# List-scheduling both attentions of a hybrid decoder with their transfers, and moving half of a second output projection into the attention ahead of it

## The chip, the cores and the metric

The kernel runs on one core of one Trainium2 chip. The metric is the device time of one execution in microseconds (us). A core has a matrix engine, TensorE (PE; its weight loads are shown as PEld), a vector engine (DVE), a scalar engine (ACT), a general engine, GpSimd (POOL), and SyncE (SP), whose queue issues all transfers of this kernel.

## What is computed

A decoder trunk of two layers over 1024 tokens of width 1024, in float32:

```python
for l in range(2):
    h = rms_norm(x, attn_norm[l])
    if l == 0:   # 12 heads of 64 in 2 groups: compressed, selected and window branch, gated sum
        o_mix, q_mem = nsa_mixer(h, a_w_in, ...)
    else:        # 12 heads: causal softmax over q k^T + decay, K, V and gates from one shared projection
        hs = rms_norm(x, kv_norm) @ w_kv_shared
        o_mix, q_mem = forgetting_attention(h @ b_w_in, hs), ...
    o_mem = memory_attention(q_mem, mem, ...)          # 4 heads over 256 memory tokens
    x = x + concat(o_mix, o_mem) @ w_o[l]
    x = x + conv_ffn(rms_norm(x, ffn_norm[l]), ...)    # 1024 -> 2 x 2816, conv of 3, gate, -> 1024
return rms_norm(x, final_norm)
```

With 1024 tokens there are 16 blocks to select from and 16 are selected, so the selected branch is plain causal attention.

## The kernel before

**Products.** Every float32 operand is split into an upper part (rounded, `hi`, made by ACT) and the rest (`lo`, made by DVE or POOL). `mm3` makes a product of three matmuls, hi x hi, hi x lo, lo x hi (L255 to L257). In attention the two parts of a query or key of 64 rows lie one above the other in one tile of 128 rows, so that two matmuls (`score`, L340) make the three products.

**Stages of the profiled execution**, about: layer 0's projections (0 to 165 us), attention 0 (165 to 600), output projection 0 (to 720), the FFN (to 1400) in a scheme that saves matmuls by sums of blocks, the shared values of layer 1 (to 1480), attention 1 (to 1770), output projection 1 (to 1880), the second FFN and the final norm (to 2506).

**A unit of attention** is one head and one half of the queries (512 columns). Its steps: load the tiles; `score`; `maximum` on DVE (L370, or L357 for a memory head); `exponent` on ACT; `sums` and `normalise`; then per group of key blocks a transpose on PE (`turn_p`, L460), the split of its result (`upper_p`, ACT, L471; `lower_p`, DVE, L474) and the product with the values (`value`, L484). Results go to DRAM (`ob` to `od`, upper and lower part separately), and are loaded, added on POOL and split as operands `oT` of the output projection (`operand`).

**Attention 0** is written by a planner. `Plan` holds tasks with an engine, a cost, what they depend on, a priority, and buffers that they take and give back; `run` simulates the engines and calls the tasks' functions in the order of their simulated starts. PE, ACT, DVE and POOL keep that order. Transfers are tasks of cost 0 on "SP", their landing a fixed delay on the dependency (4 to 9 us), and SP's instructions stand where the framework puts them. `SHIFT` moves single tasks' priorities. Between the units' tasks stand, as filler for PE, the projections of queries to come (`rope_tasks`, `plain_tasks`), and from unit -8 on one half of the output projection (`half`): the k-tiles 0 to 3 (`EARLY`) by the first 512 columns, added to `x` and stored as `xh`. `out_proj` then does the other four k-tiles for these columns, and all eight for the rest. The attention's normalising is POOL's (L424 to L428).

**Attention 1** (`attention`) follows fixed slots: `pace` sets at which step each group of scores starts, scores are `lead` steps ahead, values `lag` steps behind, and the filler (14 projections of keys and queries, `load_block` and `plain_proj`) is spread evenly up to unit -5. Normalising is DVE's (L430). The weights come with 512-byte rows, and each is split in 8 pieces with its gain (L283 on ACT, L284 on DVE). When the last unit starts, `w_o` is loaded; when the filler is done, an operand is loaded every fourth step, the rest at the end. There is no half product: `out_proj` does eight k-tiles for all columns.

**Transfers.** Parts and heads lie apart in DRAM, so tiles are loaded in pieces: `queries0` 8 DMAs for two tiles, `keys0` 4, a memory unit 4 for its queries (L952), a unit of attention 1 two for `qq`, two for `qx`; a head there two for `kk`, two for `ky`, one for `vv`.

```python
def queries0(self, pool, h, c):
    q = [self.sb(pool, [P, CH], F32R, f"qq{i}", 2) for i in range(2)]
    for i in range(2):
        for half in range(2):
            for x in range(2):
                p0 = (i ^ x) * HD + half * 32
                self.nc.sync.dma_start(f32(q[x][p0:p0 + 32, :]), self.qd0[i, half, h * 32:(h + 1) * 32, c * CH:(c + 1) * CH])
```

Of the kernel before, what the change touches and what calls it, by code (L numbers as in the profile page):

```python
# [18 lines left out]
P = 128  # L19
# [24 lines left out]
class Plan:  # L44
# [20 lines left out]

    def can(self, t):
        free, held = self.free, self.held
        for a in t["acq"]:
            if a == "tp":

                if held.get("tp", 0) > 2 or free["psb"] < (1 if held.get("o") else 2):
                    return False
            elif a == "pb":
                if free["psb"] < 2 or held.get("pb", 0) > (0 if "psa" in held else 1):
                    return False
            elif free["psb" if a == "o" else a] < t["acq"].count(a):
                return False
        return True
# [59 lines left out]
class Trunk:  # L138
# [180 lines left out]
    def score(self, it):  # L319
        nc, br, s = self.nc, it["br"], self.psa()  # L320
        it["s"] = s
        for ii, o, n in it["grp"]:
# [10 lines left out]
            for q, k in zip(br["q"], br["k"]):  # L333
# [77 lines left out]
    def normalise_all(self, u, i0, i1):  # L411
        self.sums(u, i0, i1)
        for br in u["branches"][i0:i1]:
            for ii in br["pt"]:
                self.normalise(br, ii)

# [72 lines left out]
    def pace(steps, items):  # L489


        t = [0.0]
        for st in steps:
            t.append(t[-1] + 0.11 * st["n"] + sum(2 * max(0.11, 0.057 * len(q[2])) for q in st["ps"]))
        size = [0.4 + 0.0012 * sum(n for _, _, n in it["grp"]) for it in items]
        rate, at = t[-1] / sum(size), 10 ** 9
        due, early = 10 ** 9, -10 ** 9
        for it in items:
            early = it["early"] = max(early, it["early"])
        for it, w in reversed(list(zip(items, size))):  # L500
            due = min(due - rate * w, t[it["due"]] if it["due"] >= 0 else it["due"])
            k = int(due) if due < 0 else max(i for i in range(len(steps)) if t[i] <= due)
            at = it["at"] = min(at, max(k, it["early"]))
        assert all(it["early"] <= it["at"] for it in items)

    def attention(self, ap, l, od, units, work, spare, lead=4, lag=2, lead_work=2):
# [3 lines left out]
        units = list(units)  # L510
        steps, items, users = [], [], {}
        for k, u in enumerate(units):
            u["start"] = len(steps)
            steps += self.value_steps(u)
        ends = {id(q[0]): k for k, st in enumerate(steps) for q in st["ps"]}
        for k, u in enumerate(units):
            its, brs = [], u["branches"]
            for br in brs:
                tag, _, bufs = br["p"]
                same = users.setdefault(tag, [])  # L520
                br["early"] = ends[id(same[-bufs])] if len(same) >= bufs else -10 ** 9
                same.append(br)
            scored = brs if len(brs) == 1 else brs[0:2]
            for i, br in enumerate(scored):
                early = max(b["early"] for b in (br, br.get("joint", br)))
                due = next(k for k in range(u["start"], len(steps)) if any(q[0] is br for q in steps[k]["ps"])) - lead
                its += [{"u": u, "br": br, "grp": g, "first": j == 0, "load": False, "early": early, "due": due} for j, g in enumerate(self.groups(br))]
                its[-1]["norm"] = (i, len(brs) if br is scored[-1] else i + 1)
            its[0]["load"] = True
            items += its  # L530
        self.pace(steps, items)
        n_fill = units[-spare]["start"] if spare else len(steps)
        total, owed, done = sum(n for _, n, _ in work), 0.0, set()
        work = [[name, gen] for name, _, gen in work]
        later, halves, whole, oT = {}, [], [], []

        def operand():

            if not oT:
                oT.extend(self.hpair() for _ in range(2))  # L540
            c, kt = whole.pop(0)
            raw = self.wraw([P, 2, CH])
            self.nc.sync.dma_start(raw, od[c][:, kt * P:(kt + 1) * P, :].rearrange("s p q -> p s q"))
            self.nc.gpsimd.tensor_tensor(raw[:, 0], raw[:, 0], raw[:, 1], ALU.add)  # L544
            self.split(raw[:, 0], oT[c][0][:, kt, :], oT[c][1][:, kt, :])

        def after(k, slot, f):
            later.setdefault((k, slot), []).append(f)

        def run(k, slot):  # L550
            for f in later.pop((k, slot), ()):
                f()

        def advance():
            nonlocal total
            total -= 1
            if next(work[0][1], 0) == 0:
                done.add(work.pop(0)[0])

        def begin(k, it):  # L560
            if it["load"]:
                while not set(it["u"]["needs"]) <= done:
                    advance()
                it["u"]["load"]()
            self.score(it)
# [1909 lines left out]
```

## Time and profile before

| | us |
|---|---|
| median of 3 runs | 2505.82 |
| lowest, highest | 2503.11, 2507.7 |
| profiled execution | 2507.87 |
| its span | 2506.1 |
| PE busy | 2439.7 (97%) |
| DVE, ACT, POOL busy | 1839.2, 1347.1, 843.3 |
| chain that ended last: PE, DVE, DMA, ACT | 85%, 5%, 4%, 3% |

The profile is one execution. Busy times are sums over an engine's instructions; a matmul's time runs from its start to its modelled end, and matmuls overlap, so that a full PE shows in how closely they start, not in the busy share alone. "PEclk" is the share of full clock that the matrix engine was granted. A row of waits has the engine, line and tile that waited, who released it, the sum, the number of times and the longest. In a time line, the number in brackets is the idle time ahead of an instruction, with its releaser. "SPq" is SP's queue, where a DMA waits until its buffers are free, and those behind it with it.

### The profile page before, as it was taken

To read this page: it belongs to the slowest core of one execution; us is meant where nothing else is said; L and a number is where in the kernel's file an instruction comes from. 1 tells how busy PE (TensorE), PEld (TensorE's weight loads), DVE (VectorE), ACT (ScalarE), POOL (GpSimd) and SP (SyncE) were. 2 spreads that over 40 slices of the span, in tenths; PEclk is the share of its full clock that TensorE was granted. 3 is DMA by queue.
4 is the path that set the end of the run, shared out by engine and by line. 5 is a ranking of instruction groups with operands and counts; after the bars stand their busy time and mean duration, and the time that the engine had idled before them with its cause. 6 is when DMAs were issued, how large, how long until landed. Compare 5 with 4: busy or idle time off the path is not lost.

```text
span 2506.1 us, 35521 instructions
## 1 busy us (share of the span) xinstructions
PE 2439.7 (97%) x12215; PEld 2048.1 (82%) x12215; DVE 1839.2 (73%) x3066; ACT 1347.1 (54%) x2564; POOL 843.3 (34%) x742
## 2 busy tenths in 40 slices
PE   8989999989999999999999999999999999999998
PEld 7778888877778888888889887887778888888887
DVE  4778777875678777788666477878386788778766
ACT  4458777885354444454455266757244454444444
POOL 2755555584145545520000000000234455451001
PEclk9989999999999999999999999999999999999999
DMA  8663343355423323366336467666622233338423
GB/s 273 231 216 84 98 132 94 109 169 175 148 75 109 105 93 114 101 240 226 101 119 184 150 181 196 181 189 185 208 90 92 97 102 109 101 102 309 169 93 126
DMA packets 290284, 368.18 MB, mean 147 GB/s; under 512 B 30808, under 2 KB 160696, under 8 KB 290104
## 3 DMA queue, kind: packets, MB, share of 16 engines
q1 hardware_dynamic: 290104, 365.91, 46.0%
q8 instruction: 97, 1.59, 0.3%
q14 instruction: 83, 0.68, 0.1%
HBM read 252.38 MB, written 113.45 MB: 146 GB/s over the span
## 4 chain that ended last, share of the span: by engine, by line
PE 85%; DVE 5%; DMA 4%; ACT 3%; issue 2%; POOL 1%; SPq 0%; POOLq 0%; ACTq 0%; DVEq 0%
PE psa L255 13%; PE psa L256 13%; PE psa L257 13%; PE psb L255 10%; PE psb L256 10%; PE psb L257 10%; PE psa L340 6%; PE psb L484 5%; PE psb L460 5%; PE psb L1711 1%; DVE pt L474 1%; ACT pt L471 1%; DMA wr<-in_w_r_dram 1%; ACT ps L383 1%; DVE ps L370 0%
## 5 line engine op out<-in xcount | busy, mean ns | idle before, releaser
L2205 DVE SCALAR_TENSOR_TENSOR v<-u,cw,v 128x1023 f32<-128x1023 f32 (+1 forms) x176 | 274.0, 1557 | 68.8 <-ACT v L2203 68.6
L474 DVE TENSOR_TENSOR pt<-psb,pt 128x512 fp32r<-128x512 f32 (+2 forms) x380 | 244.7, 660 | 81.0 <-ACT pt L471 78.5
L176 ACT ACTIVATE wh<-wr 128x512 fp32r<-128x512 f32 (+1 forms) x210 | 155.7, 742 | 255.4 <-PE psb L257 107.5
L471 ACT ACTIVATE pt<-psb 128x512 fp32r<-128x512 f32 (+2 forms) x380 | 213.9, 576 | 129.8 <-PE psb L460 94.3
L2203 ACT ACTIVATE v<-u,cw 128x1024 f32<-128x1024 f32 x88 | 109.6, 1246 | 310.3 <-DVE u L2192 297.1
L177 DVE TENSOR_TENSOR wl<-wr,wh 128x512 fp32r<-128x512 f32 (+1 forms) x210 | 196.3, 936 | 99.6 <-ACT wh L176 99.2
L484 PE MATMUL psb<-pt,vv 128*128 128x512 f32 (+2 forms) x864 | 249.6, 362 | 8.1 <-DVE pt L474 5.0
L255 PE MATMUL psa<-hT,wh 128*128 128x512 f32 x592 | 231.2, 391 | 4.9 <-ACT rb L1098 3.8
L257 PE MATMUL psa<-hT,wl 128*128 128x512 f32 x592 | 230.6, 390 | 0.0
L256 PE MATMUL psa<-hT,wh 128*128 128x512 f32 x592 | 230.6, 390 | 0.0
L223 POOL TENSOR_TENSOR rs<-ss,consts 128x1 f32<-128x1 f32 x28 | 17.1, 613 | 545.4 <-DVE ss L221 545.4
L340 PE MATMUL psa<-kk,qq 128*128 128x512 f32 (+4 forms) x792 | 176.7, 339 | 6.4 <-DVE stat L370 5.0
L484 PEld LDWEIGHTS psb<-pt,vv 128*128 128x128 f32 x864 | 147.6, 192 | 27.9 <-DVE pt L474 8.7
L383 ACT ACTIVATE ps<-ps,stat 128x128 f32<-128x128 f32 (+1 forms) x192 | 147.4, 770 | 29.7 <-DVE stat L370 28.6
L544 POOL TENSOR_TENSOR wr<-wr 128x512 f32<-128x512 f32 x16 | 20.8, 1301 | 410.7 <-ACT pt L471 292.6
L370 DVE CUSTOM_DVE_ANT_0 ps<-psa,caub 128x128 f32<-128x128 f32 (+1 forms) x192 | 138.7, 750 | 23.6 <-PE psa L340 20.6
L460 PE MATMUL psb<-consts,ps 128*128 128x128 f32 x928 | 148.8, 279 | 2.8 <-DVE pt L474 2.2
L2098 POOL TENSOR_TENSOR ws<-wr 128x512 f32<-128x512 f32 x44 | 77.9, 1770 | 216.6 <-DMA wr<-in_w_up_dram 178.4
L255 PE MATMUL psa<-hx,wh 128*128 128x512 f32 x368 | 144.0, 392 | 0.5 <-ACT u L2195 0.5
L256 PE MATMUL psa<-hx,wh 128*128 128x512 f32 x368 | 143.6, 390 | 0.0
L257 PE MATMUL psa<-hx,wl 128*128 128x512 f32 x368 | 143.3, 390 | 0.0
L255 PE MATMUL psb<-wh,hT 128*128 128x512 f32 (+2 forms) x352 | 132.7, 379 | 10.7 <-ACT wh L1039 8.2
(357 smaller groups left out, 6946.0 us busy)
## 6 DMA issues: line engine op xcount, KB each, us to landing
wr<-in_w_up_dram SPq DMA_DIRECT2D x88, 512.0 KB
wr<-gd SPq DMA_DIRECT2D x154, 256.0 KB
gd<-v SPq DMA_DIRECT2D x88, 256.0 KB
gd<-gs SPq DMA_DIRECT2D x66, 256.0 KB
o<-ob SPq DMA_DIRECT2D x128, 128.0 KB
wr<-o SPq DMA_DIRECT2D x32, 512.0 KB
hT<-in_w_down_dram SPq DMA_DIRECT2D x64, 256.0 KB
qd<-st SPq DMA_DIRECT2D x56, 256.0 KB
```

The costliest lines, as they stand in the source:

```text
L176: nc.scalar.activation(hi, src, AF.Copy)
L177: (low or nc.vector).tensor_tensor(lo, src, f32(hi), ALU.subtract)
L255: mm(out, lh, rh, start=first, stop=False, skip_group_check=more)
L256: mm(out, lh, rl, start=False, stop=False, skip_group_check=more)
L257: mm(out, ll, rh, start=False, stop=last, skip_group_check=more)
L340: nc.tensor.matmul(out, w, rhs, start=b not in banks[:i], stop=b not in banks[i + 1:])
L383: nc.scalar.activation(p, p, AF.Exp, bias=st[:, 0, ii:ii + 1], scale=-1.0, accum_out=st[:, 1, ii:ii + 1])
L460: nc.tensor.transpose(tp[0:kb, x:x + P], br["pt"][ii][:, o:o + kb], self.ident)
L471: self.nc.scalar.activation(st["hi"], st["src"], AF.Copy)
L474: self.nc.vector.tensor_tensor(st["lo"], st["src"], f32(st["hi"]), ALU.subtract)
L484: self.nc.tensor.matmul(u["o"][:, iis[0] * P:iis[0] * P + w], br["v"](j), t[:, x:x + w], start=st["begin"] and first and i == 0, stop=st[" ...
L2205: nc.vector.scalar_tensor_tensor(v[:, d:], u[:, :S - d], cw[:, tap, i:i + 1], v[:, d:], ALU.mult, ALU.add)
```

## The change

1. **Transfers are planned.** `Plan.dma` makes a DMA a task of 0.5 us on an engine "DQ", landing 1.8 us + KB/230 after. Each load, each store (outputs, `st`, `xh`) is such a task with a due time; a unit's `loads` are separate tasks. SP is added to the engines whose order is the plan's. `SHIFT` is written anew for layer 0 and added for layer 1.
2. **Attention 1 is planned** by the same `planned` with the lead of layer 0; `pace`, `attention`, `plain_proj` and `normalise_all` go. Its normalising goes to POOL (with a gate of ones). Its projections are `gain_tasks`: load, times gain on POOL, `hi` on ACT in one piece, `lo` on POOL. The first two weights are made during the shared values' stage (`ready`).
3. **Half product in layer 1**: `xh[1]`, as in layer 0.
4. **Layouts.** Columns of weights are interleaved by head (host side; new inputs `w_k1`, `w_q1`, `one`), so that a head's rows have one stride in DRAM. Queries are stored in three parts (hi, lo, hi; the third is one more store per half chunk), so that both tiles are one DMA of 128 rows each; keys likewise. In layer 1 a head has 132 rows: lo, hi (queries) or hi, lo (keys), and four rows for the gates and ones, so that `qx` and `ky` are one DMA of 68 rows each. Values are stored with parts interleaved, and the unit's output of 128 rows leaves in one DMA.

```diff
+    def dma(self, kb, fn, deps, prio, acq=(), rel=(), key=None):
+        return self.add("DQ", 0.5, fn, deps, prio, acq, rel, key=key), 1.8 + kb / 230.0
...
             elif a == "pb":
-                if free["psb"] < 2 or held.get("pb", 0) > (0 if "psa" in held else 1):
+                if free["psb"] < 2 + held.get("pb", 0):
...
-    def attention(self, ap, l, od, units, work, spare, lead=4, lag=2, lead_work=2):
...
-            deps = [(done[n], 6.0) for n in u["needs"]]
...
-            ld = pl.add("SP", 0.0, u["load"], deps, 0.0)
...
+            for part, kb, fn in u["loads"]:
+                deps = [s_last[k - 2] if k > 1 else None] if part == "q" else [x for i in u.get("takes", ()) for x in ((w_last if part == "v" else s_last)[i],)]
+                deps += [x for n in u["needs"] for x in done[n]]
...
+                    got.setdefault(part, []).append(pl.dma(kb, fn, deps, due - (2 if part == "v" else 4), key=("d", k)))
...
-                for i in range(2):
-                    self.nc.sync.dma_start(od[c][i, head * HD:(head + 1) * HD, :], ot[i * HD:(i + 1) * HD, :])
...
+                self.nc.sync.dma_start(od[c][head * HD:(head + 1) * HD].rearrange("r i s -> (r i) s"), u["ob"])
...
-        with self.tc.manual_schedule(engines={eng.PE, eng.Activation, eng.DVE, eng.Pool}):
+        with self.tc.manual_schedule(engines={eng.PE, eng.Activation, eng.DVE, eng.Pool, eng.SP}):
             pl.run()
...
-                for i in range(2):
-                    d = dma(256, lambda i=i, half=half: nc.sync.dma_start(dst[i, half, 0:P, cs], f32(x["s", half][:, i, :])), [p], at, (), ["st"] if i else ())
+                for i in range(2 + n):
+                    d = dma(256, lambda i=i, half=half: nc.sync.dma_start(dst[0, i, half].rearrange("r h s -> (r h) s")[:, cs], f32(x["s", half][:, i % 2, :])), [p], at, (), ["st"] if i == 1 + n else ())
...
-        for i in range(2):
-            for half in range(2):
-                p0, r0 = i * HD + half * 32, (b * NG + g) * 32
-                self.nc.sync.dma_start(f32(kk[p0:p0 + 32, :, 0:P]), self.kd0[i, half, r0:r0 + 32, :].rearrange("r (t n) -> r t n", n=P))
+        self.nc.sync.dma_start(f32(kk[:, :, 0:P]), self.kd0[0, :, :, :, b * NG + g, :].rearrange("i f r (t n) -> (i f r) t n", n=P))
...
+    def queries0(self, pool, h, c, i):
+        q = self.sb(pool, [P, CH], F32R, f"qq{i}", 2)
+        self.nc.sync.dma_start(f32(q), self.qd0[h // 4, i:i + 2, :, :, h % 4, c * CH:(c + 1) * CH].rearrange("i f r s -> (i f r) s"))
         return q
...
-        st = self.sb(pool, [P, 7, 2, HD], F32R, "sv1", 2)
+        st = self.sb(pool, [P, 7, HD, 2], F32R, "sv1", 2)
...
-            return self.attention(ap, 1, od, units, work, 5)
+            return self.planned(ap, 1, od, units, works, 8, 5, self.xd, ap, (("xh", 2), ("xh", 2)))
...
+        def gain():
+            self.nc.gpsimd.tensor_tensor(x["raw"], x["raw"], g.rearrange("p (k o) -> p k o", o=1).to_broadcast([P, KT, P]), ALU.mult)
+        def hi():
+            x["w"] = self.whl([P, KT, P])
+            self.nc.scalar.activation(x["w"][0], x["raw"], AF.Copy)
+        def lo():
+            self.nc.gpsimd.tensor_tensor(x["w"][1], x["raw"], f32(x["w"][0]), ALU.subtract)
...
-                br = {"spans": self.causal(c, self.m_cau), "kb": P, "gate": None, "p": t_s[c], "on": "dve"}
...
+                br = {"spans": self.causal(c, self.m_cau), "kb": P, "gate": ones, "p": t_s[c], "on": "pool"}
...
+                        nc.sync.dma_start(f32(ky[h % 2][0:E, :]), kd[HD:HD + E, :])
...
+                        nc.sync.dma_start(f32(qx[c][0:E, :]), self.qd1[h // 2, HD:HD + E, h % 2, cs])
...
-        self.xh = {0: self.dp.tile([S, CH], F32, name="xh0")}
+        self.xh = {l: self.dp.tile([S, CH], F32, name=f"xh{l}") for l in range(2)}
```

Here `E` is 68, `P` 128, `HD` 64, `CH` 512.

More of the change, by code (lines that the diff above doesn't have):

```diff
@@ L488, in pace @@
     @staticmethod
[L489 to L504, printed above, removed]
@@ L506, in attention @@
-    def attention(self, ap, l, od, units, work, spare, lead=4, lag=2, lead_work=2):
[L510 to L565, printed above, removed]
-            after(k + 1, "max", lambda: self.maximum(ap, it))
-            after(k + 1, "exp", lambda: self.exponent(ap, it))
-            if "norm" in it:
-                after(k + 2, "norm", lambda: self.normalise_all(it["u"], *it["norm"]))
-        def finish(k, u):
-            h, c = u["at"]
-            def out():
-                ot = self.sb(ap, [P, CH], F32, "ob", 2)
-                self.nc.scalar.activation(ot, u["o"], AF.Copy)
-                for i in range(2):
-                    self.nc.sync.dma_start(od[c][i, h * HD:(h + 1) * HD, :], ot[i * HD:(i + 1) * HD, :])
-                halves.append((c, h // 2))
-                if halves.count((c, h // 2)) == 2:
-                    whole.append((c, h // 2))
-            after(k + 1, "exp", out)
-        first = min(it["at"] for it in items)
-        for k in range(first, len(steps) + lag + 4):
-            st = steps[k] if 0 <= k < len(steps) else None
-            run(k, "max")
-            if st:
-                self.turn_p(ap, st)
-                self.upper_p(ap, st)
-            run(k, "exp")
-            if st:
-                self.lower_p(st)
-            run(k, "norm")
-            while items and items[0]["at"] <= k:
-                begin(k, items.pop(0))
-            if k < 0 and lead_work and items:
-                for _ in range(lead_work):
-                    if work:
-                        advance()
-            if st and k < n_fill:
-                owed += max(total, 0) / (n_fill - k)
-                while owed >= 1 and work:
-                    owed -= 1
-                    advance()
-            if 0 <= k - lag < len(steps):
-                for part in range(len(steps[k - lag]["t"])):
-                    self.value(steps[k - lag], part)
-                if steps[k - lag]["end"]:
-                    finish(k, steps[k - lag]["u"])
-            if not work and whole and k % 4 == 0:
-                operand()
-            if k == units[-1]["start"]:
-                w_o = self.load_block(self.a["w_o"][l], [(0, CH)])
-        while whole:
-            operand()
-        assert not work and not later
-        return oT, w_o
@@ L955, in mem_units @@
-                yield {"branches": [br], "load": load, "needs": [need(h)], "at": (NH + h, c)}
-    def plain_proj(self, pool, h, wcol, dst, m, scale=None):
-        for c in range(2):
-            ps = self.psb()
-            yield from self.proj_c(ps, wcol, h, c)
-            st = self.sb(pool, [P, 2, CH], F32R, "st", 2)
-            self.split(ps, st[:, 0, :], st[:, 1, :], scale)
-            for i in range(2):
-                self.nc.sync.dma_start(dst[i, m * P:(m + 1) * P, c * CH:(c + 1) * CH], f32(st[:, i, :]))
+                q = {}
@@ L968, in layer0_proj @@
+                loads = [] if c else [("k", 128, keys)]
+                loads += [("q", 256, lambda i=i, query=query: query(i)) for i in range(2)]
+                loads += [] if c else [("v", 256, values)]
+                br.update(pairs=lambda q=q, kv=kv: [(q[i], kv["k"]) for i in range(2)], v=lambda j, kv=kv: kv["v"][:, j, :])
+                yield {"branches": [br], "loads": loads, "needs": [need(h)], "at": (NH + h, c)}
     def layer0_proj(self, cpool):
@@ L1632, in units0 @@
                     brs[1]["joint"] = brs[2]
[L1634 to L1643 removed]
+                    q = {}
```

425 lines of the change are left out of this document (238 added, 187 removed), and 24 rows, old and new, of the table SHIFT.

## The prediction

> **What bounds the kernel now.** I read the page's first part, then the windows by stage, the waits of TensorE (PE), and the time lines of PE and of SyncE's queue (SP) where PE stood idle.
>
> ```profile
> span 2506.1 us, 35521 instructions
> PE 2439.7 (97%) x12215; PEld 2048.1 (82%) x12215; DVE 1839.2 (73%) x3066; ACT 1347.1 (54%) x2564; POOL 843.3 (34%) x742
> ```
>
> PE bounds the whole; the other engines matter only where they hold it up. Where is that? The windows give, per stage, PE's busy time with its count, PEld, DVE, ACT and POOL likewise, then the granted PE clock, DMA share and GB/s:
>
> ```profile
> core 0: us, PE busy (x) PEld busy (x) DVE busy (x) ACT busy (x) POOL busy (x), PEclk, DMA share, GB/s
> 165.00:600.00 435.00, 418.21 (x2604) 364.68 (x2605) 335.30 (x933) 339.86 (x845) 266.08 (x355) 0.98 0.41 118
> 600.00:720.00 120.00, 117.27 (x577) 95.02 (x576) 73.59 (x100) 44.62 (x73) 36.42 (x32) 1.00 0.43 145
> 800.00:1200.00 400.00, 399.38 (x1757) 329.05 (x1756) 317.30 (x314) 188.43 (x249) 158.73 (x94) 1.00 0.43 144
> 1480.00:1700.00 220.00, 217.18 (x1195) 180.47 (x1194) 170.67 (x430) 146.51 (x369) 3.90 (x3) 1.00 0.65 185
> 1700.00:1780.00 80.00, 72.07 (x354) 57.19 (x353) 61.56 (x121) 46.83 (x94) 16.92 (x13) 0.91 0.69 210
> 1780.00:1880.00 100.00, 98.03 (x481) 80.09 (x480) 62.89 (x83) 35.15 (x57) 23.92 (x20) 1.00 0.36 126
> ```
>
> The FFN (row 800 to 1200) is full: 400 us for 1757 matmuls, 0.228 us each, at full clock. Nothing is to be had there, and the change does not touch it. What can be had lies in attention 0 (165 to 600: 16.8 us idle, clock 0.98), in the tail of attention 1 (1700 to 1780: 7.9 us idle, clock 0.91, so 7 us more), and in the seam ahead of attention 0. The edits aim at these places. [...]
>
> **The change, part by part.**
>
> *Seam, projections to attention 0.* Key and query tiles come in one DMA each, where they were pieces of 32 rows (`keys0` 4 DMAs, `queries0` 8 for two tiles); the price is one more store per `turn` half, 4 in all.
>
> ```profile
> 144.73 5.76 SPq L1611 DMA_DIRECT2D qq<-qd  x8
> 150.59 1.60 SPq L1493 DMA_DIRECT2D wr<-in_w_mem_kv_dram  x1
> 153.63 0.47 SPq L1549 DMA_DIRECT2D vmem<-xl  x1
> 154.21 1.97 SPq L868 DMA_DIRECT2D wr<-in_w_r_dram  x2
> 167.05 3.52 PE L340 MATMUL psa<-kk,qq 128*128 128x192 f32 x14 [4.81 <-DVE stat L370]
> 157.00:167.00 10.00, 3.95 (x32) 3.55 (x30) 4.73 (x12) 5.40 (x9) 6.65 (x3) 0.88 0.80 279
> 167.00:172.00 5.00, 4.95 (x19) 4.63 (x20) 3.01 (x19) 3.66 (x15) 0.79 (x1) 0.57 1.00 331
> ```
>
> The last memory weights and the rope weights stand on SP behind the 8 query pieces. Two issues at 0.47 instead of 5.76 let them go 4.8 us sooner, less 4 stores x 0.47 = 1.9 ahead: 2.9. PE loses 6.1 us idle plus 0.43 x 5 = 2.1 us of clock here, 8.2 in all. I take 3.5 gained (2.9 with its share of clock). Ends: 8 gained; 2 lost, if the extra stores hold up the queue's other loads.
>
> *Attention 0.* Already planned; now SP is in the plan with 0.5 us an issue and 1.8 us + KB/230 to landing, a unit's loads are 2 issues instead of 8 (memory units 2 instead of 4), the store of a half product is a task of its own, and the outputs leave in 1 DMA, not 2.
>
> ```profile
> PE psa L340 <- DMA qq<-qm: 8.4, 5, 3.1
> 422.89 1.11 SPq L725 DMA_DIRECT2D o<-ob  x2
> 424.09 2.46 SPq L952 DMA_DIRECT2D qq<-qm  x4
> 428.29 2.35 PE L340 MATMUL psa<-mk,qq 128*128 128x256 f32 x8 [3.07 <-DMA qq<-qm]
> 420.00:440.00 20.00, 16.93 (x93) 14.74 (x92) 11.39 (x26) 13.40 (x40) 12.92 (x18) 0.83 0.40 112
> 540.00:550.00 10.00, 6.16 (x37) 5.61 (x35) 5.58 (x10) 4.67 (x15) 9.20 (x12) 0.84 0.71 210
> 590.00:600.00 10.00, 7.98 (x48) 5.91 (x48) 7.06 (x15) 6.70 (x13) 7.01 (x9) 1.00 0.84 251
> ```
>
> PE waited 8.4 us for the memory queries, which stood on SP behind stores; the clock lost with it is 0.17 x 20 = 3.4 and 0.16 x 10 = 1.6. Together 13.4 us. Late next is POOL (9.20 of 10 us busy at 540), so I take 12. Ends: 4 (only the 4 us that fewer issues give directly), and 17 (13.4 and the remaining 3.6 us of idle: 16.8 - 8.4 - the 4.8 counted at the seam). The end at 590 (2 us idle, for the last operand) stays.
>
> *Attention 1.* It leaves the fixed slots of `attention` for `planned`. Three things move.
>
> (1) Normalising goes from DVE to POOL, and the weights' gains and low parts too.
>
> ```profile
> L430 DVE TENSOR_SCALAR ps<-ps,stat 128x1024 f32<-128x1024 f32 x10 | 7.5, 746 | 0.0
> L430 DVE TENSOR_SCALAR ps<-ps,stat 128x128 f32<-128x128 f32 x10 | 3.9, 388 | 0.2
> L284 DVE SCALAR_TENSOR_TENSOR wl<-wr,gcol,wh 128x128 fp32r<-128x128 f32 x56 | 16.9, 343 | 3.0 <-ACT wh L283 3.0
> L428 POOL TENSOR_SCALAR ps<-ps,stat,gates 128x1024 f32<-128x1024 f32 x11 | 13.4, 1215 | 0.0
> L428 POOL TENSOR_SCALAR ps<-ps,stat,gates 128x128 f32<-128x128 f32 x11 | 5.0, 452 | 0.9
> L426 POOL TENSOR_TENSOR pm<-pm,stat 128x1024 f32<-128x1024 f32 x8 | 15.1, 1896 | 0.3
> L875 POOL TENSOR_TENSOR wl<-wr,wh 128x1024 fp32r<-128x1024 f32 x2 | 4.8, 2397 | 0.1
> L749 POOL TENSOR_TENSOR wr<-wr 128x512 f32<-128x512 f32 x12 | 15.5, 1291 | 1.9 <-DMA wr<-o 1.9
> ```
>
> A head has 8 tiles of 128 to 1024 columns. On POOL, between 452 and 1215 ns, they make 8 x 0.833 = 6.7 us, 80 us for 12 heads; 8 memory units x 1.9 = 15; 12 weights x (1.9 + 2.4) = 52 (2 of the 14 are made before the stage); 16 operands x (1.29 + 1.29, as sum and low part) = 41. About 190 of 300 us: POOL was idle here (3.9 + 16.9), so it is cover that exists, but in the last third (4 heads 27 + 41) it is near full. DVE is freed of 14 x 8 x 0.343 = 38 and 12 x 8 x 0.567 (between 388 and 746 ns) = 54 us of its 232. None of this is on PE's path while POOL keeps up: priced 0, up to 11 lost in the tail otherwise.
>
> (2) The half product: 8 row tiles x 4 k-tiles x 3 = 96 matmuls x 0.228 = 21.9 us leave 1780 to 1880 and fill the tail.
>
> (3) The operand and `w_o` loads are planned ahead.
>
> ```profile
> 1731.86 12.22 SPq L272 DMA_DIRECT2D wr<-in_w_o_dram  x3
> 1745.30 0.58 PE L484 MATMUL psb<-pt,vv 128*128 128x256 f32 x1 [1.14 <-DVE pt L474]
> 1740.00:1750.00 10.00, 7.59 (x32) 5.56 (x33) 9.30 (x17) 7.35 (x13) 0.00 (x0) 0.74 0.50 158
> 1750.00:1755.00 5.00, 5.00 (x19) 4.07 (x19) 4.33 (x6) 2.43 (x4) 1.28 (x1) 0.50 0.82 226
> ```
>
> Here SP stood 12 us in `w_o` loads, DVE was full (9.30 of 10) and PE waited on it in pieces of about 1 us until its clock halved. How much comes back? At the rate of 1480 to 1700, 1195 / 220 = 5.43 matmuls a us, the tail's 354 need 65.2 us instead of 80: 14.8 back. The last operand's wait stays, as in attention 0: -2.0. Of the 2.8 us idle in 1480 to 1700, half. 14 in all. Ends: 3 (14 less 11, POOL full), and 17.6 (14.8 + 2.8). The matmuls' own order costs nothing: as many, of the same sizes.
>
> The Trainium skill speaks on the clock ("TensorE: Matmul & The Clock Gate", Part 1: The HAM clock gate): the half clock follows an idle window of about 3.4 us. By that rule alone the tail's waits of 1 us would have cost no clock, 7 us less would come back, and the time would be 2484. The row 1750 to 1755 says otherwise, clock 0.50 after waits of at most 1.14; the same page's "A second HAM failure mode" has such short idles throttle too, and with that the trace agrees.
>
> *Output projection 1.* Its first half shrinks by the 21.9 us already counted as moved, and the loads of its second half have less time. Layer 0 has that form: 2.7 us idle in 600 to 720, against 2.0 in 1780 to 1880. I take -1 (0 to -3).
>
> *Interleaved columns, the shared-value layout, the `one` rows.* Stores with a stride of two in ACT and DVE: in the stages where they lie PE is dense and DVE has room (317 of 400 us in 800 to 1200), so 0.
>
> ```profile
> L177 DVE TENSOR_TENSOR sv<-psb,sv 128x384 fp32r<-128x384 f32 x8 | 4.4, 549 | 12.5 <-ACT sv L176 12.5
> ```
>
> Without that cover, 16 such pairs of stores at 1.5 times this price would cost 16 x 0.27 = 4 us an engine.
>
> **Sum.** 3.5 + 12 + 14 - 1 = 28.5 us. The profiled execution took 2507.9 us (span 2506.1): 2479.4. It stands 2.05 above the median of 2505.8, so 2477. Bounds: -2 + 4 + 3 - 3 = 2 gained, 2504; 8 + 17 + 17.6 = 42.6 gained, 2463.
>
> **Rivals.**
>
> *POOL takes DVE's place in attention 1.* For it: in the last third 68 us are POOL's, of some 78 (8 units, at the pace found below), and at 540 a POOL at 9.20 of 10 stood beside PE idle. Against: norms are due five steps ahead. It costs the 11 above and delays the half product's operands by a few: 2490.
>
> *The memory queries stay late.* Their wait is store, then load through DRAM; if the store, not the queue, is what ends last, 9 of attention 0's 12 stay: 2486.
>
> *Slower: the 68-row tiles.* The new `ky` and `qx` loads have 68 rows (64 and 4 that carry the gates and ones), where 64 and 2 came apart.
>
> ```profile
> 1705.23 4.24 DMA kk<-kd
> L576 ACT ACTIVATE ob<-psb 128x512 f32<-128x512 f32 x25 | 14.8, 595 | 9.3 <-PE psb L484 9.3
> 1780.00:1790.00 10.00, 10.00 (x46) 8.29 (x45) 2.07 (x3) 0.00 (x0) 0.00 (x0) 1.00 1.04 384
> ```
>
> All engines moved 384 GB/s. If such a tile got only a quarter of them, 96 GB/s, the 272 KB of `ky` take 2.8 us instead of 0.7, and what stands behind it on those engines is late as well. With 4.24 us for `kk` today it lands after 6.3 us. From 1500 to 1742 there were 25 units (one `ob` each), 9.7 us a unit; the load may start one unit ahead, so 3.4 us are in hand; SP's other work decides. If every head's scores then came 3 us late and every unit's queries 1.5, 12 x 3 + 24 x 1.5 = 72 us, half of it under the projections: 36 lost, and 2513. It decides where it takes more than the 28.5 gained, at 0.8 of that lateness: 2.4 us a head.
>
> The Trainium skill's "DMA: Bandwidth & Descriptors", section "Why a DMA increments its semaphore by 16 and not by 1", states such a rule: a DMA runs on the largest number up to 16 of engines that divides its slowest dimension. For 68 that is 4, for 64 and 128 it is 16. No row of before shows it.
>
> *More than I think*: the planner also saves switches between kinds of matmul, and all idle goes: 2457.
>
> **How the numbers follow.** The sum's way, 2477 give or take 10: 0.50. POOL full 0.14, queries late 0.12, more 0.10; slower 0.10; nothing to speak of 0.04. A measurement of this kernel tells about 0.2% (5 us) from no change. Faster 0.85, same 0.05, slower 0.10. The range 2457 to 2503 leaves out the slow case and half of the best.
>
> **What would show it.** Right: no wait of L340 for `qq<-qm` in attention 0 and clock 1.00 around its memory units; attention 1's tail at clock near 1 with the half product's matmuls in it and POOL at 60 to 90%; SP without a 10 us stand. Wrong: PE idle behind POOL's L428 tiles or behind `ky` and `qx` in attention 1; a seam as wide as now; FFN rows that move at all.

## The result and the profile after

2538.61 us median of 4 runs (2538.17 to 2543.56) against 2505.86 for the kernel before (2503.11 to 2507.7): ratio 1.0136, 95% interval 1.0119 to 1.0154. The change made the kernel 33 us slower, where 2477 was forecast, and above the range's end of 2503.

Lines that the text below needs were renumbered: `score` is L344, `turn_p` L458, `upper_p` and `lower_p` L469 and L472, `value` L482, `normalise` L424 and L426, `ob` L596 and its store L599, the operand's load and sum L622 and L625, the memory queries' load L849, the stores of keys and queries of layer 1 L1794, and in a unit of attention 1 `kk` L1824, `ky` L1826, `vv` L1830, `qq` L1836, `qx` L1838. In experiments that add lines these numbers are up to 2 higher, in two of them 19 to 22.

The page of the changed kernel begins:

```profile
span 2536.4 us, 34946 instructions
PE 2442.7 (96%) x12215; PEld 2051.2 (81%) x12215; DVE 1766.0 (70%) x2787; ACT 1331.0 (52%) x2466; POOL 1016.8 (40%) x922
```

As many matmuls, busy for 3 us more, in a span that is 30 us longer: PE stands idle, and no other engine is near full (DVE and ACT are less busy than before, POOL has 40% where it had 34). Where? Both kernels make the same 12215 matmuls, so windows from 0 that hold equally many of them say how far one is ahead. First the kernel before (the count in the first bracket):

```profile
0.00:165.00 165.00, 140.51 (x799) 124.07 (x799) 104.68 (x146) 78.17 (x125) 82.81 (x61) 0.97 0.77 254
0.00:720.00 720.00, 676.00 (x3978) 583.77 (x3979) 513.57 (x1177) 462.65 (x1042) 385.31 (x446) 0.98 0.49 154
0.00:1420.00 1420.00, 1375.11 (x7171) 1172.13 (x7172) 1028.87 (x1824) 792.37 (x1549) 589.71 (x572) 0.99 0.46 145
0.00:1880.00 1880.00, 1822.38 (x9506) 1540.78 (x9507) 1362.27 (x2555) 1052.27 (x2148) 634.45 (x608) 0.99 0.49 153
```

and the changed one:

```profile
0.00:163.00 163.00, 140.95 (x799) 124.67 (x799) 104.32 (x146) 77.91 (x123) 82.58 (x61) 0.96 0.77 260
0.00:703.50 703.50, 670.93 (x3978) 581.28 (x3979) 511.80 (x1177) 464.46 (x1042) 385.32 (x446) 0.99 0.49 163
0.00:1404.20 1404.20, 1370.25 (x7171) 1169.70 (x7172) 1030.95 (x1784) 786.87 (x1512) 601.96 (x581) 0.99 0.45 149
0.00:1911.00 1911.00, 1825.85 (x9508) 1544.16 (x9509) 1286.51 (x2276) 1036.38 (x2050) 808.00 (x788) 0.98 0.48 155
```

2.0 us ahead at the start of attention 0, 16.5 after output projection 0, 15.8 at 7171 matmuls, shortly before layer 1's attention starts, and 31 behind after output projection 1. So the seam and attention 0 won 16.5 (forecast 15.5), and attention 1 with its output projection lost 47 (forecast: 13 won). Stretches of the changed kernel; the second is the end of attention 0 (it stands at 583.2 with the 3403 matmuls that the kernel before has at 600), the third the first loads of attention 1:

```profile
420.00:440.00 20.00, 19.17 (x118) 15.72 (x117) 10.64 (x17) 11.28 (x25) 7.21 (x6) 1.00 0.43 141
573.80:583.20 9.40, 9.25 (x58) 7.59 (x57) 7.94 (x12) 5.96 (x11) 7.43 (x9) 1.00 0.63 211
1404.20:1481.70 77.50, 63.20 (x313) 51.37 (x311) 29.04 (x64) 34.77 (x80) 37.01 (x33) 0.93 0.59 174
1480.00:1600.00 120.00, 105.75 (x539) 86.28 (x540) 55.84 (x123) 62.92 (x142) 46.33 (x48) 0.94 0.57 166
1600.00:1700.00 100.00, 93.88 (x497) 78.28 (x496) 42.73 (x86) 48.02 (x114) 31.40 (x35) 1.00 0.52 152
1700.00:1780.00 80.00, 65.30 (x344) 54.05 (x343) 45.12 (x104) 49.43 (x111) 38.48 (x45) 0.91 0.66 204
```

The places in attention 0 are mended, the end at 590 too, which the prediction had left as it was. From 1404 on PE idles all along, 14 of 77.5 us, 14 of 120, 6 of 100, 15 of 80, with the clock down in all but the third, while DVE and POOL are busy for 31 to 56% of the time. Of the 47 us, 17 are lost in the first of these stretches: it ends at 1481.7 with 7482 matmuls, which the kernel before has at 1480. PE's waits in 1370 to 1810:

```profile
PE psa L344 <- DMA qq<-qd: 24.1, 10, 5.9
PE psa L344 <- DMA qx<-qd: 14.3, 12, 2.3
```

Before, no wait of `score` for a load stood in this stage. One such wait, read from SP's time line, from the chain (its `qx` row is start, length, what) and from windows of 5 us:

```profile
1489.91 8.04 SPq L599 DMA_DIRECT2D o<-ob  x3
...
1499.47 1.19 SPq L1824 DMA_DIRECT2D kk<-kd  x2
1500.70 0.48 SPq L1826 DMA_DIRECT2D ky<-kd  x1
1501.29 0.33 SPq L1836 DMA_DIRECT2D qq<-qd  x1
1501.65 0.33 SPq L1838 DMA_DIRECT2D qx<-qd  x1
1502.08 0.47 SPq L1830 DMA_DIRECT2D vv<-vd  x1
```

```profile
1501.65 12.17 DMA qx<-qd
```

```profile
1500.00:1505.00 5.00, 5.00 (x24) 4.14 (x23) 0.00 (x0) 0.00 (x0) 1.88 (x2) 1.00 1.03 261
1505.00:1510.00 5.00, 2.60 (x12) 1.83 (x10) 0.69 (x1) 0.60 (x1) 1.03 (x1) 1.00 1.08 205
1510.00:1515.00 5.00, 1.60 (x6) 1.42 (x7) 0.00 (x0) 0.00 (x0) 0.00 (x0) 0.60 0.74 177
```

PE's time line has the two waits:

```profile
1511.27 0.47 PE L344 MATMUL psa<-kk,qq 128*128 128x128 f32 x1 [3.67 <-DMA qq<-qd]
1513.87 0.47 PE L344 MATMUL psa<-ky,qx 128*128 128x128 f32 x1 [2.13 <-DMA qx<-qd]
```

SP stood 8 us at three output stores; then all tiles of a head went out within 4 us, the DMA engines were full (share 1.03 and 1.08), the 128-row `qq` came 10 us after its issue, and the `qx` of 68 rows (136 KB) after 12.17. Before, `kk` (256 KB) landed after 4.24. PE did 4.2 us of work in 10, and its clock fell to 0.60. Two things stand in this picture: a slow transfer, and a burst of loads behind a queue that stood. The experiments take them apart.

### The profile page after: what moved, and what is told of

The parts are those of the page before. It is cut to its first block, busy times and chain, and to the rows that moved or that the text cites. A ratio compares the mean times of both kernels' runs of the same rounds, so it can differ in the third digit from the quotient of the medians.

```text
span 2536.4 us, 34946 instructions
## 1 busy us (share of the span) xinstructions
PE 2442.7 (96%) x12215; PEld 2051.2 (81%) x12215; DVE 1766.0 (70%) x2787; ACT 1331.0 (52%) x2466; POOL 1016.8 (40%) x922
## 4 chain that ended last, share of the span: by engine, by line
PE 84%; DMA 7%; DVE 4%; ACT 2%; issue 1%; SPq 1%; POOL 1%; POOLq 0%; ACTq 0%; DVEq 0%
PE psa L259 13%; PE psa L260 13%; PE psa L261 13%; PE psb L259 10%; PE psb L261 10%; PE psb L260 10%; PE psa L344 6%; PE psb L458 5%; PE psb L482 5%; DMA qx<-qd 3%; PE psb L1606 1%; DMA kk<-kd 1%; ACT pt L469 1%; DMA qq<-qm 1%; DVE pt L472 1%
## 5 line engine op out<-in xcount | busy, mean ns | idle before, releaser
L472 DVE TENSOR_TENSOR pt<-psb,pt 128x512 fp32r<-128x512 f32 (+2 forms) x380 | 244.1, 660 | 92.4 <-ACT pt L469 89.8
L469 ACT ACTIVATE pt<-psb 128x512 fp32r<-128x512 f32 (+2 forms) x380 | 214.3, 576 | 132.9 <-PE psb L458 77.3
L482 PE MATMUL psb<-pt,vv 128*128 128x512 f32 (+2 forms) x864 | 266.7, 366 | 7.1 <-ACT pt L469 3.2
L344 PE MATMUL psa<-kk,qq 128*128 128x512 f32 (+4 forms) x792 | 178.9, 340 | 28.9 <-DMA qq<-qd 24.1
L482 PEld LDWEIGHTS psb<-pt,vv 128*128 128x128 f32 x864 | 148.1, 191 | 22.7 <-ACT pt L469 7.0
L344 PEld LDWEIGHTS psa<-kk,qq 128*128 128x128 f32 x792 | 127.6, 195 | 46.1 <-issue 16.0
L2071 POOL TENSOR_TENSOR ws<-wr 128x512 f32<-128x512 f32 x44 | 71.3, 1621 | 214.8 <-DMA wr<-in_w_up_dram 186.5
L458 PE MATMUL psb<-consts,ps 128*128 128x128 f32 x928 | 145.0, 275 | 3.4 <-DVE pt L472 1.6
```

The lines of the kernel that those rows point to most:

```text
L344: nc.tensor.matmul(out, w, rhs, start=b not in banks[:i], stop=b not in banks[i + 1:])
L458: nc.tensor.transpose(tp[0:kb, x:x + P], br["pt"][ii][:, o:o + kb], self.ident)
L469: self.nc.scalar.activation(st["hi"], st["src"], AF.Copy)
L472: self.nc.vector.tensor_tensor(st["lo"], st["src"], f32(st["hi"]), ALU.subtract)
L482: self.nc.tensor.matmul(u["o"][:, iis[0] * P:iis[0] * P + w], br["v"](j), t[:, x:x + w], start=st["begin"] and first and i == 0, stop=st[" ...
```

## The experiments

Each ratio is to the kernel before, run on the same chip; its medians there were 2504.5 to 2506.7 us, so that medians of different chips compare within some 2 us. The theories that the expectations name: A, a transfer whose slowest dimension is 68 rows gets few engines; B, the 8 KB stride between the rows of the new layout; C, the loads are merely issued late; D, the filler projections store keys and queries too late; E, SP's written order in layer 1; F, the plan's cost of 0.5 us a transfer.

### The 68 rows

`ky` and `qx` in two DMAs, 64 and 4 rows (the same edit for both):

```diff
-nc.sync.dma_start(f32(ky[h % 2][0:E, :]), kd[HD:HD + E, :])
+nc.sync.dma_start(f32(ky[h % 2][0:HD, :]), kd[HD:2 * HD, :])
+nc.sync.dma_start(f32(ky[h % 2][HD:E, :]), kd[2 * HD:HD + E, :])
```

> Only the qx and ky loads change: 64 rows and 4 rows in two DMAs each instead of one of 68 rows, 36 more issues on SP. Theory A (a tile of 68 rows is carried by few DMA engines, and everything that shares them comes late): the qx landings of 8 to 13 us fall to 3 to 5, the 38 us in which TensorE waits for qq and qx go, time 2476 to 2484. Theory B (the rows of the new layout, 8 KB apart in DRAM, are what is slow): the pieces have the same stride, landings stay at 8 to 13 us, time 2530 to 2545. Theory C (the planner issues the loads too late in attention 1, because its landing figure is too small): 36 more issues make it later still, 2540 to 2560.

2506.42, ratio 1.0002 (0.9992 to 1.0012): 32 us faster than the changed kernel, but 22 short of what A alone was expected to bring. The same with only `ky` cut:

> Only ky is split in 64 and 4 rows, qx stays one DMA of 68 rows. Both move the same bytes in all (12 x 272 KB and 24 x 136 KB). Theory A: half of the load on the few engines goes, and with it more than half of the lateness: 2485 to 2510, the rest of the waits at qx. If a single one of them does the harm: 2476 (ky) or 2538 (qx).

2521.98 (one run), above the 2485 to 2510 expected; PE's wait for `qx` is still there, 12.3 us in all where it was 14.3.

Or one DMA of 80 rows, the 12 more being zeros:

```diff
-        E = HD + 4
+        E = HD + 16
```

> qx and ky are loaded as 80 rows in one DMA, the DRAM tensors have 12 more rows of zeros per pair of heads, filled once by two DMAs. 18% more bytes in these loads, as many issues as in the changed kernel. Theory A (80 divides by 16, 68 only by 4): landings of 3 to 5 us, time 2474 to 2482, as fast as the split or a little faster. Theory B (stride) and theory C (late issue): 2538 or above, since more bytes move in the same way.

2504.6, ratio 0.9997 (0.9988 to 1.0007), 23 above the expected range. And 72 rows:

> The same with 72 rows, which divides by 8 but not by 16. Theory A: landings in between, nearer to the fast side since the rate doubles (the engines that qx and ky use are shared by the others, so the wait falls more than by half): TensorE's waits for qq and qx 5 to 15 us instead of 38, time 2480 to 2505. Theory that any count that is not 64 or 128 is slow in the same way: 2538. Theories B and C: 2538 or above.

2508.53 (one run). So 68 rows 2538.6, 72 rows 2508.5, 80 rows 2504.6, 64 and 4 rows 2506.4; half of it mended, 2522. The row count stands as a cause, at 32 to 34 us in this kernel. B falls: with 80 rows the stride is the same and the bytes are more. C falls as the whole cause: no store or load was moved. That few engines are the reason is A's own claim. No run counts them, but the changed kernel's trace bears it out where the burst is over. SP issued a `qx` at 1519.56 (its row in the chain) and nothing more until 1525.75; from 1522 on (second row) the share is 0.28 and the rate 89 GB/s, about a quarter of the 1.04 and 384 in the prediction's row at 1780, and the tile still came only at 1528:

```profile
1519.56 8.46 DMA qx<-qd
```

```profile
1522.00:1526.00 4.00, 4.00 (x22) 3.23 (x20) 2.10 (x5) 2.65 (x6) 2.24 (x4) 1.00 0.28 89
```

PE's waits with 80 rows are down from 38.4 to 11.2 us, and although the same burst is there, no `qx` landing in the trace is longer than 9.2 us (third row, from the view of that tile):

```profile
PE psa L344 <- DMA qq<-qd: 9.6, 4, 4.4
PE psa L344 <- DMA qx<-qd: 1.6, 4, 0.5
DMA to landing us min/median/max: 4.3/6.2/9.2
```

But this only brings back the time before, where attention 0 alone had won 16. A second cause remains in attention 1.

### What else is late in attention 1

The next four stand on 80 rows (2504.6). Filler projections due 12 steps ahead of their first need:

```diff
+            if l:
+                need = min(u["start"] for u in units if w["name"] in u["needs"]) - 12
+                prio = [min(p, need - (w["n"] - 1 - i)) for i, p in enumerate(prio)]
```

> On the 80-row version: in layer 1 each projection's due steps are pulled ahead so that it ends 12 steps before the first unit that needs it (before, the 14 projections are spread evenly: the pair for heads 2 and 3 is due at step 34 of 96, its unit starts at step 24, and so for heads 4 to 7). Theory D (the loads stand behind projections that are due too late, and then come all at once): TensorE's waits for qq and qx in attention 1 fall from 11 us to under 4, and the time by 10 to 20 us, to 2485 to 2495. Theory E (the hand-written order of SP is what stops the loads, whatever the due times): no change, 2500 to 2510. Theory F (the transfers are too many at once for the DMA engines): no change or a few us.

2536.47, ratio 1.0132 (1.0115 to 1.0149). D falls: PE's waits for `qq` and `qx`, which were to go under 4 us, rose from 11.2 to 16.2. But it does not fall cleanly: the edit moves the whole plan, and `SHIFT` had been fitted to the plan as it was. What that fit is worth:

```diff
-              1: {"e0": {3: -9, 7: 7, 13: 4, 25: 9},
...
+              1: {}}
```

> On the 80-row version: the table of single shifts for layer 1 is empty. If the shifts, found for another cost, are what harms attention 1: faster, 2485 to 2500. If they help on the chip: slower, 2510 to 2525. Theories D, E and F have no part in it: within 5 us of 2505.

2536.69 (two runs), ratio 1.0129 (1.0109 to 1.0149): 32 us, as much as e5 lost. An edit that changes the plan's order is therefore read with care here; those below leave it, where they can. SP left to the framework's order in layer 1:

```diff
-manual_schedule(engines={eng.PE, eng.Activation, eng.DVE, eng.Pool, eng.SP}):
+manual_schedule(engines={eng.PE, eng.Activation, eng.DVE, eng.Pool} | (set() if l else {eng.SP})):
```

> On the 80-row version: in layer 1 SP is left out of the engines whose order is the plan's, so that the framework places the transfers, as it did in the kernel before. Theory E: 2485 to 2495, the stands of SP of up to 20 us on output stores go. Theory D or F: no gain, 2500 to 2520, since the loads wait for the same projections.

2489.89 (two runs, 2486.6 and 2493.1), ratio 0.9942 (0.9921 to 0.9964). E stands: 15 us, and PE's waits for `qq` and `qx` from `qd` are down to 0.4 us. The plan with a transfer's size in its cost instead:

```diff
-        return self.add("DQ", 0.5, fn, ...
+        return self.add("DQ", max(0.5, kb / 300.0) if self.bw else 0.5, fn, ...
```

> On the 80-row version: in layer 1 the plan counts a transfer as KB/300 us of the DMA queue (0.85 us for 256 KB, 1.7 for 512) instead of 0.5 for any size, so that it knows the rate. Theory F (bursts of 13 loads at a DMA share of 1.0 to 1.1 make a load of 256 KB land after 8 to 10 us): 5 to 15 us faster than 2505. Theories D and E: within 5 us of it, either way, since the order within a burst may change.

2499.05, ratio 0.9981 (0.9971 to 0.9992): with F's edit the kernel is 5.5 us faster as long as SP keeps the plan's order, though this edit too changes the plan. On top of e6 it is not:

> e6 (80 rows, SP free in layer 1) with the plan of layer 1 counting a transfer on the DMA queue at its size / 300 (KB, us) instead of 0.5 us, as in e7. If the plan's compute order then expects transfers where they land: the hole of PE at 1700 to 1720 (ACT behind an operand load, 7 us) shrinks, 2483 to 2487. The rival: with SP free the order of the loads is no longer the plan's, so its costs no longer matter, or SHIFT fits the changed plan less well: 2488 to 2498.

2494.93, ratio 0.9953 (0.9936 to 0.9970), 5 us slower than e6: the rival.

### Do the two causes add?

e6's edit on the changed kernel, 68 rows as they are:

> The changed kernel with its 68-row tiles as they are, and with SP out of the written order in layer 1 alone, as in e6 (which had 80 rows and took 2489.9). If the two causes are apart and add (few engines for 68 rows, 33 us; SP's written order, 15 us): 2538.6 - 15 = 2523, with PE waiting for qq and qx from DRAM as in the changed kernel. The rival: the 68-row tiles cost so much only because the written order issues the loads late behind output stores; with SP free they are issued early enough to hide a landing of 8 to 13 us: 2490 to 2500.

2499.2, ratio 0.9984 (0.9974 to 0.9994). The rival holds, they do not add:

| median us | SP in the written order | SP free in layer 1 |
|---|---|---|
| 68 rows | 2538.6 | 2499.2 |
| 80 rows | 2504.6 | 2489.9 |
| 64 + 4 rows | 2506.4 | 2485.9 |

Freeing SP is worth 39 us with the slow tiles and 15 to 21 without; the tiles cost 32 to 34 us in the written order and 9 to 13 out of it. In the stretch shown above, SP of e9 issues a few loads at a time:

```profile
1500.49 0.32 SPq L1836 DMA_DIRECT2D qq<-qd  x1
1500.90 0.28 SPq L1838 DMA_DIRECT2D qx<-qd  x1
...
1512.70 0.45 SPq L1824 DMA_DIRECT2D kk<-kd  x1
```

and PE waits for `qx` 2.6 us in all where it was 14.3. A `qx` issued there at 1508.43, of 68 rows and 136 KB as before, is in the chain with

```profile
1508.43 4.47 DMA qx<-qd
```

The last field of the table:

> SP free in layer 1 with ky and qx as 64 + 4 rows in two DMAs each (e1_split's tiles, no zero rows) in place of e6's 80 rows. If only the number of engines counts: 2490 within 4, though it issues 36 more loads (0.33 each on SP). The rival, that SP is short of time in attention 1: 2494 to 2500.

2485.86, ratio 0.9922 (0.9902 to 0.9943), the lowest median of all, 4 us below 2490 and so a little beyond the range expected; e6's two runs do not tell the two apart. The 36 more issues cost nothing that shows. With equal counts as above, it is 13.3 us ahead of the kernel before at 7171 matmuls and 20 us ahead after output projection 1:

```profile
0.00:1406.70 1406.70, 1371.38 (x7171) 1170.54 (x7172) 1033.71 (x1784) 786.89 (x1512) 604.32 (x582) 0.99 0.45 150
0.00:1860.00 1860.00, 1814.28 (x9508) 1536.95 (x9509) 1290.38 (x2277) 1035.80 (x2050) 809.18 (x788) 0.99 0.49 160
```

### Which part of SP's order is it?

The output stores of the changed kernel's layer 1 issued from ACT's queue:

```diff
-                self.nc.sync.dma_start(od[c][...], u["ob"])
+                (self.nc.scalar if l else self.nc.sync).dma_start(od[c][...], u["ob"])
```

> The changed kernel (68 rows, SP in the written order) with one edit: in layer 1 the 24 or so output stores o<-ob of attention are issued from ACT's queue, which makes ob itself, and no longer stand in SP's written order. If SP's stands behind those stores are what makes the loads late: SP's waits at L599 go, and much of the 39 us comes that freeing SP altogether gave with 68 rows (2538.6 to 2499.2): 2500 to 2515. The rival: it is the order of the loads among themselves and the stores of the projections (L1796) that count: 2530 to 2540.

2535.54, ratio 1.0115 (1.0091 to 1.0140): the rival, 3 us. The longest of SP's waits in 1400 to 1800, in the changed kernel

```profile
SPq L599 <- ACT ob L596: 65.6, 20, 8.9
SPq L1794 <- ACT st L1779: 41.0, 10, 11.4
```

and in e13:

```profile
SPq L1794 <- ACT st L1779: 88.9, 13, 24.7
```

SP now stood at the next stores in its order. So all stores of layer 1 were moved up to 10 us later in it (never behind the first task that needs them); loads and compute keep their order:

```diff
+            for i, t in enumerate(order):
+                if t.get("store"):
+                    stop = min([pos[o["id"]] for o, _ in t["out"]] + [end])
+                    j = i + 1
+                    while j < stop and order[j]["at"] < t["at"] + self.late:
+                        j += 1
+                    key[t["id"]] = (j, 0)
```

> The changed kernel (68 rows, SP in the written order) with one edit: once layer 1's plan is made, every store (o<-ob, kd<-st, qd<-st) is moved up to 10 us later in SP's written order, though never behind the first task that needs it. The loads keep their order among themselves and the compute engines theirs. If what costs 39 us is SP standing at stores whose data come later than planned, with loads behind them: most of it returns, 2500 to 2515, and SP's waits at L599 and at the st stores shrink. The rival: the order of the loads themselves, or their waits for free tiles: 2530 to 2540.

2541.47, ratio 1.0144 (1.0123 to 1.0164), 1.5 us above even the rival's range, and with 80 rows

> The same move of layer 1's stores with 80 rows (e2_pad80, 2504.6). Standing at stores as the cause: most of the 15 us that freeing SP gave, 2490 to 2496. The rival: 2502 to 2506.

2517.98, ratio 1.0052 (1.0032 to 1.0072): slower by 13 than 2504.6, and 12 above the rival's range. Neither theory had this. In e16 PE's waits for `qq` and `qx` did fall, from 38.4 to 11.4 us, but others came (here L477 is `turn_p`, L363 `score`, L616 writes `ob`):

```profile
PE psa L363 <- DMA qx<-qd: 8.6, 7, 2.1
...
PE psb L477 <- ACT ob L616: 7.9, 3, 6.0
```

and one of ACT's own waits that does not stand among the changed kernel's longest:

```profile
ACT ob L616 <- DMA o<-ob: 35.4, 7, 11.5
```

`ob` and `st` have two buffers; a store that leaves later holds its buffer longer, and ACT stands at the next `ob` with PE's work behind it. So a store that stands early makes the loads behind it wait, and a late one its buffer; that no place in between would do is not shown. Nor does the length of SP's stands decide by itself: at the stores of `ob` and `st` SP waited 138 us in 1400 to 1800 in the changed kernel, 97 in e16 and 96 in e9, which is 42 us faster than e16. That the written order costs 15 to 39 us and the framework's does not is shown; which part of it costs how much is open.

### The other terms of the prediction

SP free in layer 0's attention too, on e6:

> e6 (80 rows, SP free in layer 1) with SP free in layer 0's attention too. The prediction put 12 us of attention 0's gain on SP standing in the plan together with fewer issues. If the plan of SP is what gained there: the waits for memory queries come back, 2490 + 8 to 12 = 2498 to 2502. The rival: the fewer and larger transfers (2 issues a unit for 8) gained it, and the written order of SP does nothing good in either layer: 2487 to 2493.

2492.72, ratio 0.9950 (0.9932 to 0.9967): the rival; SP's place in the plan won nothing in attention 0 that is clear of e6's spread. And e6 with the pieces back:

```diff
-        self.nc.sync.dma_start(f32(q), self.qd0[h // 4, i:i + 2, ...
+        for j in range(4):
+            self.nc.sync.dma_start(f32(q[j * n:(j + 1) * n, :]), self.qd0[h // 4, i + j // 2, j % 2, ...
```

> e6 with the query loads of layer 0's attention in 4 DMAs of 32 rows a tile, and the memory queries (both layers) in 2 of 64, as in the kernel before; same tiles, same plan, same place in SP's order, 3 and 1 more issues at 0.47 each. If fewer issues gained attention 0's 12 us and the seam: 2490 + 8 to 14 = 2498 to 2504, with PE waiting for qq. The rival: the plan of loads ahead of their use did it, whatever their number: 2490 within 4.

2500.29, ratio 0.9982 (0.9964 to 1.0000): 10 us lost, within the 8 to 14 expected. The traces say where: e6 and e15 reach the end of the seam (799 matmuls) at 162.4 and 161.7, but the end of attention 0 (3403) at 582.6 and 592.7. So fewer and larger query transfers are what won most of attention 0 (the memory queries were cut in two likewise, in both layers), and the seam has no share in it. Normalising back on DVE, at the plan's places:

```diff
+        elif br.get("dve"):
+            nc.vector.tensor_scalar(br["pt"][ii], br["pt"][ii], r[:, ii:ii + 1], None, ALU.mult)
```

> e6 with the normalising of the 24 causal units of layer 1 issued on DVE at the places that the plan gave it on POOL; plan, matmul order and all else as in e6. The step that priced the move at nothing (neither DVE nor POOL bounds): 2490 within 4. The rival that POOL is too full in the last third: the hole of PE at 1700 to 1720 shrinks and the time falls by 3 to 7, 2483 to 2487. The rival that DVE needed the relief (its 54 us and the finer waits behind it): 2496 to 2505.

2504.1, ratio 1.0001 (0.9991 to 1.0011): 14 us lost. The longest of PE's waits in 1370 to 1810 (L484 and L474 are `value` and `lower_p` here), and the tail:

```profile
PE psb L484 <- DVE pt L474: 7.7, 6, 3.5
```

```profile
1700.00:1780.00 80.00, 74.13 (x403) 61.19 (x402) 63.42 (x126) 54.18 (x113) 38.13 (x34) 0.96 0.74 228
```

It is the kind of wait that the prediction's row at 1745.30 has, and POOL, which took the work, holds PE up for 0.3 us in e6. But the place is another: in the tail PE is nearly as busy as in e6, at the same clock (75.19, below), and the loss lies ahead of it. From 7171 to 8675 matmuls, where the kernel before has 1420 to 1700, e11 took 297.7 us and e6 284.0. The 14 us are those of this plan, which was made for POOL; a plan made for DVE was not run. The half product behind all of attention 1:

```diff
+            def when(f):
+                return (lambda: later.append(f)) if l else f
```

> e6 with the half product of layer 1 (96 matmuls, 21.9 us) issued behind all of attention 1 where the plan put it between the last units; nothing is left out. If it fills holes, as the prediction had it: the tail of attention 1 shows idle PE and lost clock of 8 to 15 us again, 2498 to 2505. The rival: there was no hole left to fill, the matmuls are only displaced: 2490 within 4.

2508.42, ratio 1.0017 (1.0007 to 1.0027): 18.5 us of its 21.9 had filled holes, again in a plan made with it. In 1700 to 1780, e12 and then e6:

```profile
1700.00:1780.00 80.00, 66.07 (x324) 53.28 (x323) 39.59 (x77) 43.97 (x88) 52.23 (x50) 0.91 0.66 205
```

```profile
1700.00:1780.00 80.00, 75.19 (x377) 61.18 (x377) 43.12 (x79) 41.98 (x85) 49.64 (x48) 0.96 0.79 252
```

PE's longest wait there in e6, 1.74 us, ends at 1713.74. The chain behind it has

```profile
1703.65 9.35 DMA wr<-o
```

and ACT's time line goes on:

```profile
1712.58 0.63 ACT L628 ACTIVATE hT<-wr 128x512 fp32r<-128x512 f32 x1 [2.66 <-POOL wr L625]
```

An operand's load takes 9.35 us; POOL's sum (L625) waits for it, ACT stands at the operand's `hi` (L628), and the `upper_p` that PE needs, at 1713.11, is behind that in ACT's order.

## Why the prediction was wrong, and where it was right

**The step that failed** is "Attention 1": 14 us won there and 1 lost in the output projection became 47 lost for both. Two mechanisms did that: the row count of `ky` and `qx`, a term of the rival that was given little weight, and SP's written order, which the sum counted as a gain only.

The first was named, in the rival "Slower: the 68-row tiles", and mis-sized. It took a landing of 6.3 us, 3 us of lateness a head, half of it hidden, 36 us in all, and gave the case 0.10. Its rate was right, a quarter (96 GB/s taken, 89 measured in the stretch above). That its 36 us are near the 32 to 34 of the written order is luck: a landing measured 12.17 us where 6.3 were taken for twice the size, behind a burst that the rival did not have, and without that order the rows cost 9 to 13. The rule of the Trainium skill quoted there ("DMA: Bandwidth & Descriptors", section "Why a DMA increments its semaphore by 16 and not by 1") gives 4 engines for 68 rows and for the 4 rows of 64 + 4, 8 for 72, 16 for 64 and 80; 2538.6, 2508.5 (one run), 2506.4 (64 + 4) and 2504.6 agree with it in order. A rule that spoke so plainly against a part of the change, with no row against it, deserved more than one chance in ten.

The second was not named. Part (3) counted planned loads as a gain, and "SP without a 10 us stand" was to show it right. SP did not stand less, but elsewhere: 8.04 us at `ob`, up to 11.4 at `st`. The prediction asked of POOL what its lateness holds up, and not of SP, whose written order puts each load behind stores of results that come when they come. The order cost 15 to 21 us by itself, and made the first mechanism about three times as dear (32 to 34 us against 9 to 13); this is shown by freeing SP. That it works through loads behind late stores is read from the stretch at 1489.91 and not shown by itself, since e13, e16 and e17 did not bring the time back. A stand alone need not do harm: in attention 0 SP waited up to 14.7 us at `ob`, and the stage was won.

**Also mis-sized**: even without the two mechanisms attention 1 with its output projection won 6.7 us in e18 (20 less 13.3) where 13 were forecast, and e18 took 2485.9 us where the forecast was 2477. Its windows say where, roughly:

```profile
1700.00:1780.00 80.00, 74.63 (x380) 60.19 (x379) 44.17 (x78) 42.45 (x86) 50.83 (x49) 0.98 0.76 247
```

The tail still has 5.4 us of idle and 1.6 of clock, so 8 of the forecast 14.8 came back, and from 1406.7 to 1480 PE idled 2.0 us, where the kernel before, from 1420 to 1480, had no idle. The move of normalising to POOL, priced 0, was worth 14 us in e6's surroundings, and the half product 18.5. These two are not parts of the 6.7: each was taken out of a plan made with it, and the plan's numbers alone move the stage by 32 us (e8).

**Right**: the seam won 2.0 (forecast 3.5, from -2 to 8) and attention 0 with its output projection 14.5 (forecast 12, from 4 to 17), with clock 1.00 at 420 to 440. But attention 0's cause was split wrongly: the lower end was to be what fewer issues give, 4 us, and the rest SP's plan. e15 and e10 say 10 for the fewer query transfers and nothing for SP's place in the plan; that the total came out so near is luck in part. The FFNs stayed as they were, as expected: 16.5 us ahead became 15.8, and 31 behind ended as 30. Two terms were also summed wrongly, without weight for the result: 2.9 us with the share of clock of the prediction's own rows (8.2 for 6.1) makes 3.9 and not 3.5, and of the 4.8 us taken off as counted at the seam only 2.05 lie in the window from 165 on (the wait ends at 167.05), so that the upper end for attention 0 is near 20 and not 17.

**The other rivals.** POOL did not take DVE's place: e11 goes the other way, and POOL is busy for 48% of 1700 to 1780 in the changed kernel, below the 60 to 90 that the prediction expected. The memory queries did not stay late; of 8.4 us of waits these are left in 160 to 600:

```profile
PE psa L344 <- DMA qq<-qm: 1.8, 2, 1.2
```

The two readings of the clock gate, 7 us apart in the prediction, are not told apart further: PE's waits in the slow stretch above are 3.67 and 2.13 us, and with a wait as long as the first both have the clock fall.

## What to carry to other kernels

Look at the row count of every tile whose layout a change touches: a tile of 68 rows in one DMA cost more here than the 36 issues that it saved, and 64 + 4 rows in two DMAs did as well as 80 in one. Before SP's order is written by hand, ask of each store what stands behind it when its data come late; where loads and stores share the queue, an order that the framework makes beat the planned one by 15 to 39 us in layer 1, and was its equal in layer 0 (e10). And size a wait by the burst that it releases, not by one transfer: two faults of 15 and 9 us made 49 together.

## What the runs showed of the hardware that was not expected

The landing of one and the same transfer, 136 KB of 68 rows, went from 4.47 us (e9, where SP issued a few loads at a time) to 12.17 us (the changed kernel, in a burst with DMA share 1.03 to 1.08); the 256 KB of `kk` before took 4.24 us. In the same burst with 80 rows and 160 KB no `qx` took more than 9.2. From 68 to 72 rows, with more bytes, the kernel gained 30 us; the 4 us from 72 to 80 are not clear of the spread, since 72 rows has one run.
